# One layer of a hybrid SSD, RWKV-7 and PEER model: elementwise work of the RWKV branch moved from GpSimd to DVE and ACT

## The chip, the cores and the metric

The kernel runs on one core of a Trainium2 chip. The engines are named as in the profile: PE (TensorE; PEld is its loading of weights), DVE (VectorE), ACT (ScalarE), POOL (GpSimd) and SP, which issues most DMAs. The metric is the time of one execution in microseconds. Before the change the median of three runs is 3061.49 us (3054.85 to 3067.48).

## The reference

One inference step of a layer for a prompt of 512 tokens and eight sample tokens with states. All matrices are float32.

```python
h = rmsnorm(x, norm_mix)
z, xbc_raw, dt_raw, rw_proj, gate_m, gate_r = split_proj(h @ w_in)     # 1024 -> 11552 columns
y_m, ... = mamba_branch(z, xbc_raw, dt_raw, ...)                       # SSD scan, 32 heads of 64
y_r, ... = rwkv_branch(rw_proj, ...)                                   # RWKV-7, 16 heads of 64
x = x + (sigmoid(gate_m) * y_m + sigmoid(gate_r) * y_r) @ w_out
x = x + peer(rmsnorm(x, norm_ffn), ...)                                # 16384 experts
x = x + sigmoid(rmsnorm(x, norm_ple) @ w_ple_gate) * (p @ w_ple_proj)
```

The change lies in the RWKV branch. Its input is mixed with the row before, and then each head carries a 64 x 64 state through the tokens:

```python
xs = proj + (prev - proj) * shift_mu
r, k, v, xw, xa, xg = split(xs)
kk = normalised k * k_k ;  k = k * (1 + (a - 1) * k_a)
s = s * w + (s @ (-kk)) (x) (kk * a) + v (x) k ;   y = s @ r           # for every token
```

## The kernel before

The kernel goes through the layer in stages. Up to about 1180 us it projects `h @ w_in` in tiles of 128 columns and works off both branches from them; then come the output projections, and from about 1450 us PEER. Every float32 projection is made of three passes over split operands (`mm3`, L95 to L97): a weight tile `wraw` of 1024 x 128 is copied by ACT to `whi` (L78), DVE makes the rest `wlo` (L79), and PE runs 2 x 8 x 3 = 48 matmuls of 260 columns. `wraw`, `whi` and `wlo` have two buffers each, so a cast L78 can start only when PE has done the tile two before it.

The RWKV branch is worked through in eight groups of two heads, g = 0 to 7. In each, `rw_tile` (L413) makes r, k and v; `rwkv_in` (L518) makes the scaled vectors; `rwkv_inv` (L574) inverts small triangular blocks on DVE, in a loop over L598 and L601, with two round trips through DRAM to change the layout (the second is L602, a copy on ACT, then the DMAs L603 and L606); `rwkv_pre` (L615) does the chunk matrices; and `rwkv_chain` (L681) passes the state through eight chunks of 64 tokens. Sample tokens (`rwkv_s`, `ssd_s`) and the SSD branch (`ssd`) are interleaved with it, and projection tiles fill PE between them. Names that matter: `bb` = kk x a; `bk` = bb and k2 scaled by `di`, one instruction for each half of the partitions and each factor (L559, L560); `ck` the same with `de` (L561, L562); `di` and `dp` at L610 are the diagonal blocks and their transposes, which `mm4` (L513) takes at once; `AM` (L647, L671) is used by the chain.

A scheduler orders the instructions when the program is built: each engine gets one list, which it works off strictly in order, by estimated durations, priorities and the buffers at hand. A `pin` keeps an instruction in the order of the source. Moving an instruction to another engine therefore makes a new list on every engine.

Of the kernel before, what the change touches and what calls it, by code (L numbers as in the profile page):

```python
# [14 lines left out]
OP = mybir.AluOpType  # L15
# [15 lines left out]
def tile_hybrid(ctx: ExitStack, tc, x_prompt, x_sample, p_prompt, p_sample, state_ssm, state_conv,  # L31
# [7 lines left out]
    V, S, G, T = nc.vector, nc.scalar, nc.gpsimd, nc.tensor  # L39
# [373 lines left out]
    def rw_tile(j):  # L413

        ps = proj(W_RW + j * P, P, hT)
        raw = raw_of(ps, rwS[:, j], rtail[:, j:j + 1], 1)
        d = l2.tile([P, 2, NH], F32, name="dtmp").rearrange("p i t -> p (i t)")[:, :512]
        G.tensor_tensor(d, raw[:, 2:514], raw[:, 3:515], op=OP.subtract)
        xs = lp.tile([P, 512], F32, name=f"xs{min(j // 8, 2)}")
        V.scalar_tensor_tensor(xs, d, rows["shift_mu"][:, j:j + 1], raw[:, 3:515], op0=OP.mult, op1=OP.add)  # L420
        return xs
# [81 lines left out]
    def c8(t):  # L503
        return t.rearrange("p (c t) -> p c t", t=64)
# [13 lines left out]
    def rwkv_in(g, r, k, v, lw_):  # L518

        ps = pb()  # L520
        T.matmul(ps, lhsT=lw_[64:128, 1], rhs=xa[64:128], start=True, stop=True)
        a = full("a")
        S.activation(a, ps, AF.Tanh, scale=0.5, bias=rows["aaa_a0"][:, g:g + 1])
        S.activation(a, a, AF.Copy, scale=0.5, bias=0.5)
        ps = pb()
        for b in range(4):
            T.matmul(ps[:, b * P:(b + 1) * P], lhsT=xwaug[:, b * P:(b + 1) * P], rhs=lw_[0:65, 0], start=True, stop=True)
        lw = full("lw")
        S.activation(lw, ps, AF.Tanh, scale=0.5)
        S.activation(lw, lw, AF.Copy, scale=-0.5 * CDEC, bias=-0.5 * CDEC)  # L530
        dr, di, dp_, de = full("dr"), full("di"), full("dp"), full("de")
        for m, outs in ((cumI, ((dr, 1.0), (di, -1.0))), (cumS, ((dp_, 1.0),)), (cumC, ((de, 1.0),))):
            ps = pb()
            for b in range(4):
                T.matmul(ps[:, b * P:(b + 1) * P], lhsT=lw[:, b * P:(b + 1) * P], rhs=m, start=True, stop=True)
            for o, sg in outs:
                S.activation(o, ps, AF.Exp, scale=sg)
        drc = l2.tile([P, 8], F32, name="drc")
        V.tensor_copy(drc, dr[:, 63:512:64])

        sq = full("sq")
        S.activation(sq, k, AF.Square, scale=rows["k_k"][:, g:g + 1])
        ps = head_rs(sq, 1e-12, bd64, pb)
        kk = full("kk")
        V.scalar_tensor_tensor(kk, k, rows["k_k"][:, g:g + 1], ps, op0=OP.mult, op1=OP.mult)
        bb = full("bb")
        G.tensor_tensor(bb, kk, a, op=OP.mult)
        V.tensor_scalar(a, a, rows["k_a"][:, g:g + 1], omka[:, g:g + 1], op0=OP.mult, op1=OP.add)
        k2 = full("k2")
        V.tensor_tensor(k2, k, a, op=OP.mult)  # L550
        V.scalar_tensor_tensor(sq, r, rows["r_k"][:, g:g + 1], k2, op0=OP.mult, op1=OP.mult)
        ar = lp.tile([P, 8, 2, 64], F32, name="ar", bufs=2)
        V.scalar_tensor_tensor(ar[:, :, 0, :], c8(kk), -1.0, c8(dp_), op0=OP.mult, op1=OP.mult)
        V.tensor_tensor(ar[:, :, 1, :], c8(r), c8(dr), op=OP.mult)
        bk = lp.tile([P, 8, 2, 64], F32, name="bk")
        ck = lp.tile([P, 8, 2, 64], F32, name="ck")
        for e in range(2):
            sl = slice(64 * e, 64 * e + 64)
            V.tensor_tensor(bk[sl, :, e, :], c8(bb)[sl], c8(di)[sl], op=OP.mult)  # L559
            V.tensor_tensor(bk[sl, :, 1 - e, :], c8(k2)[sl], c8(di)[sl], op=OP.mult)  # L560
            G.tensor_tensor(ck[sl, :, e, :], c8(bb)[sl], c8(de)[sl], op=OP.mult)  # L561
            G.tensor_tensor(ck[sl, :, 1 - e, :], c8(k2)[sl], c8(de)[sl], op=OP.mult)  # L562
        return drc, sq, ar, bk, ck

    def bonus(sq, v):
# [8 lines left out]
    def rwkv_inv(g, ar, bk):  # L574

        L64 = c8(full("de"))
        lc16 = lp.tile([P, 8, 16], F32, name="lw")
        for hf in range(2):
            hs = slice(4 * hf, 4 * hf + 4)
            L = mm4(lambda ro, i: ar[ro, 4 * hf + i, 0, :], lambda ro, i: bk[ro, 4 * hf + i, ro.start // 64, :])  # L580
            V.tensor_tensor(L64[:, hs], L, b64(m64, 4), op=OP.mult)
            lm = c8(full("kk"))[:, 0:4]
            V.tensor_tensor(lm, L, b64(m16, 4), op=OP.mult)
            V.tensor_reduce(lc16[:, hs], lm.rearrange("p c (b k) -> p c k b", k=16), axis=AX.X, op=OP.add)
        ld, td = ld_d[g % 2], td_d[g % 2]
        nc.scalar.dma_start(ld.rearrange("c p k -> p c k"), lc16)
        yield
        lb = lp.tile([64, 16, 16], F32, name="a")
        pin(nc.sync.dma_start(lb.rearrange("q r k -> q (r k)"), ld.rearrange("c (z r) k -> (c z) (r k)", r=16)))
        yield  # L590
        tb = lp.tile([64, 16, 32], F32, name="sq")
        pin(V.memset(tb, 0.0))
        V.memset(tb.rearrange("p r k -> p (r k)")[:, 0:512:33], 1.0)
        tf = lp.tile([64, 16, 16], F32, name="k2")
        for j in range(15):
            tt = tf[:, j + 1:, 0:j + 1]
            sh = [64, 15 - j, j + 1]
            i = V.tensor_tensor(tt, lb[:, j + 1:, j:j + 1].to_broadcast(sh), tb[:, j:j + 1, 0:j + 1].to_broadcast(sh), op=OP.mult)  # L598
            if j == 0:
                pin(i)  # L600
            V.tensor_tensor(tb[:, j + 1:, 0:j + 1], tb[:, j + 1:, 0:j + 1], tt, op=OP.add)  # L601
        S.copy(tb[:, :, 16:32], tb[:, :, 0:16].rearrange("p r k -> p k r"))  # L602
        nc.scalar.dma_start(td.rearrange("c (z r) k -> (c z) (r k)", r=16), tb.rearrange("q r k -> q (r k)"))  # L603
        yield
        tc16 = lp.tile([P, 8, 32], F32, name="lw")
        pin(nc.scalar.dma_start(tc16, td.rearrange("c p k -> p c k")))  # L606
        yield
        T16, TT16 = c8(full("di")), c8(full("dp"))
        for q, (E_, t) in enumerate(((V, T16), (G, TT16))):
            pin(E_.tensor_tensor(t.rearrange("p c (b k) -> p c b k", k=16),  # L610
                                 tc16[:, :, None, 16 * q:16 * q + 16].to_broadcast([P, 8, 4, 16]),
                                 mb16[:, None].to_broadcast([P, 8, 4, 16]), op=OP.mult))
        yield L64, T16, TT16

    def rwkv_pre(g, v, ar, bk, ck, L64, T16, TT16):  # L615
# [21 lines left out]
        for hf in range(2):  # L637
# [30 lines left out]
                S.copy(uv[rv, e], pv[rv])  # L668
            for e in range(2):
                ro = slice(64 * e, 64 * e + 64)  # L670
                G.tensor_copy(AM[ro, e, :, 0:64], ar[ro, 4 * hf:4 * hf + 4, 0, :])  # L671
            out.append((AM, TT64, ctok, uv))
        return out

# [1042 lines left out]
```

## Time and profile before

| | |
|---|---|
| median of three runs | 3061.49 us |
| profiled execution | 3051.57 us |
| its span | 3049.9 us |
| PE busy | 2821.5 us (93%) |
| DVE busy | 2249.9 us (74%) |
| ACT busy | 988.6 us (32%) |
| POOL busy | 685.8 us (22%) |

Busy shares are taken over the whole span. [...] A line such as `PE psB L513 <- DVE bk L559` says that PE's instruction at L513, which writes psB, stood idle until DVE's instruction at L559, which writes bk, was done. In a timeline the brackets hold the idle time before an instruction and what ended it.

### The profile page before, as it was taken

What the parts mean: (1) busy time and instruction counts of PE and PEld (TensorE: products, weight loads), DVE (VectorE), ACT (ScalarE), POOL (GpSimd) and SP (SyncE); (2) the same over time, 40 slices, a digit from 0 to 9 for tenths busy, and PEclk for the clock granted to TensorE, in tenths of its full rate; (3) what the DMA queues carried; (4) which work ended last, traced back from release to release, by engine and by line L of the source; (5) the groups of instructions that cost most, each with busy time, mean ns of one, the idle gap of its engine ahead of it and who ended that gap; (6) DMA issues with size and microseconds to landing.
All of it is one profiled execution on the core that took longest, in us unless ns stands there. A gap on an engine that the chain in (4) does not pass through costs nothing. (4 is left out here: it accounts for less than half of the span.)

```text
span 3049.9 us, 52517 instructions
## 1 busy us (share of the span) xinstructions
PE 2821.5 (93%) x20188; PEld 2617.4 (86%) x20192; DVE 2249.9 (74%) x5375; ACT 988.6 (32%) x1995; POOL 685.8 (22%) x522
## 2 busy tenths in 40 slices
PE   5999999898897999998968989899999999999998
PEld 4878888777777888987968989898999999999986
DVE  5867767787777775334999999695677778878846
ACT  2333323333242322332223333232323343333332
POOL 0222231322314132210013121121222333432100
PEclk9999979998988999999989999999999999999999
DMA  3314242424334265632326768677998989988830
GB/s 87 78 41 105 76 103 60 113 60 104 73 87 113 68 153 158 198 112 93 90 61 198 245 203 245 211 241 230 315 334 303 328 302 327 337 326 313 287 119 29
DMA packets 446995, 528.15 MB, mean 173 GB/s; under 512 B 95464, under 2 KB 357243, under 8 KB 446705
## 3 DMA queue, kind: packets, MB, share of 16 engines
q1 hardware_dynamic: 386153, 377.42, 40.1%
q0 software_dynamic: 38304, 139.22, 13.5%
q10 hardware_dynamic: 22288, 8.16, 1.1%
q8 instruction: 159, 2.61, 0.4%
q14 instruction: 91, 0.75, 0.1%
HBM read 447.83 MB, written 77.14 MB: 172 GB/s over the span
## 5 line engine op out<-in xcount | busy, mean ns | idle before, releaser
L97 PE MATMUL ps<-hhi,wlo 128*128 128x260 f32 (+1 forms) x1456 | 444.6, 305 | 1.7 <-DVE wlo L79 1.7
L96 PE MATMUL ps<-hlo,whi 128*128 128x260 f32 (+1 forms) x1456 | 444.4, 305 | 0.0
L95 PE MATMUL ps<-hhi,whi 128*128 128x260 f32 (+1 forms) x1456 | 443.8, 305 | 0.6 <-DVE rsa L122 0.3
L97 PE MATMUL psA<-h2h,ul 128*128 128x392 f32 x1024 | 354.1, 346 | 24.8 <-DVE ul L1500 24.4
L95 PE MATMUL psA<-h2h,uh 128*128 128x392 f32 x1024 | 365.7, 357 | 0.2 <-ACT uh L1499 0.2
L96 PE MATMUL psA<-h2l,uh 128*128 128x392 f32 x1024 | 354.6, 346 | 0.0
L97 PE MATMUL av<-ah,vl 128*128 128x392 f32 x1024 | 351.5, 344 | 1.9 <-DVE vl L79 1.9
L95 PE MATMUL av<-ah,vh 128*128 128x392 f32 x1024 | 348.9, 341 | 3.3 <-ACT vh L78 3.2
L96 PE MATMUL av<-al,vh 128*128 128x392 f32 x1024 | 349.6, 341 | 0.9 <-DVE al L79 0.9
L95 PEld LDWEIGHTS ps<-hhi,whi 128*128 128x128 f32 (+1 forms) x1456 | 286.6, 197 | 13.9 <-issue 6.8
L96 PEld LDWEIGHTS ps<-hlo,whi 128*128 128x128 f32 (+1 forms) x1456 | 286.6, 197 | 12.7 <-issue 6.0
L97 PEld LDWEIGHTS ps<-hhi,wlo 128*128 128x128 f32 (+1 forms) x1456 | 286.3, 197 | 12.6 <-issue 4.0
L1453 POOL DMA_INDIRECT gr<-in_peer_v_dram,e x128 | 184.3, 1440 | 367.9 <-DVE o L1468 349.7
L1453 POOL DMA_INDIRECT gr<-in_peer_u_dram,e x128 | 125.3, 979 | 499.8 <-DVE junk L1462 448.2
L78 ACT CAST vh<-vr 128x1024 fp32r<-128x1024 f32 x128 | 134.3, 1051 | 315.8 <-PE av L96 121.3
L97 PEld LDWEIGHTS psA<-h2h,ul 128*128 128x128 f32 x1024 | 196.7, 192 | 27.4 <-DVE ul L1500 26.3
L78 ACT CAST whi<-wraw 128x1024 fp32r<-128x1024 f32 (+1 forms) x115 | 119.9, 1043 | 292.9 <-PE ps L96 250.5
L95 PEld LDWEIGHTS psA<-h2h,uh 128*128 128x128 f32 x1024 | 196.7, 192 | 0.9 <-ACT uh L1499 0.9
L96 PEld LDWEIGHTS psA<-h2l,uh 128*128 128x128 f32 x1024 | 197.3, 193 | 0.0
L79 DVE TENSOR_TENSOR vl<-vr,vh 128x1024 fp32r<-128x1024 f32 x128 | 156.2, 1222 | 55.4 <-ACT vh L78 52.2
L95 PEld LDWEIGHTS av<-ah,vh 128*128 128x128 f32 x1024 | 192.9, 188 | 3.9 <-ACT vh L78 3.5
L97 PEld LDWEIGHTS av<-ah,vl 128*128 128x128 f32 x1024 | 192.9, 189 | 2.5 <-DVE vl L79 2.5
(635 smaller groups left out, 6498.9 us busy)
## 6 DMA issues: line engine op xcount, KB each, us to landing
ur<-in_peer_u_dram SPq DMA_DIRECT2D x128, 512.0 KB
vr<-in_peer_v_dram SPq DMA_DIRECT2D x128, 512.0 KB
wraw<-in_w_in_dram SPq DMA_DIRECT2D x90, 512.0 KB
Gt<-G_d SPq DMA_DIRECT2D x32, 784.0 KB
G_d<-stg SPq DMA_DIRECT2D x12, 2048.0 KB
ge_d<-ge SPq DMA_DIRECT2D x112, 196.0 KB
gl<-ge_d SPq DMA_DIRECT2D x112, 196.0 KB
wraw<-in_w_out_ssm_dram SPq DMA_DIRECT2D x16, 512.0 KB
```

Source lines behind the costliest of these rows:

```text
L78: S.copy(hi, raw)
L79: eng.tensor_tensor(lo, raw, f(hi), op=OP.subtract)
L95: T.matmul(out, lhsT=a[0], rhs=b[0], start=start, stop=False)
L96: T.matmul(out, lhsT=a[0], rhs=b[1], start=False, stop=False)
L97: T.matmul(out, lhsT=a[1], rhs=b[0], start=False, stop=stop)
L1453: pin(G.indirect_dma_start(out=t, out_offset=None, in_=(peer_u, peer_v)[s_ // P][0], in_offset=bass.IndirectOffsetOnAxis(ap=e3[:, s_ % P:s ...
```

## The change

Six places of the RWKV branch change engine. DVE now makes the difference of the shifted rows (L418, 26 times), `bb` (L547, 8 times), `ck` (L561 and L562, 32 times) and `dp` (L610, 8 times); ACT makes the copies into `AM` (L671, 32 times). POOL keeps its work on the sample tokens (L836, L837, L842, L916, L920) and of the SSD branch (L994, L1008).

```diff
--- before.py
+++ after.py
@@ -415,7 +415,7 @@
         ps = proj(W_RW + j * P, P, hT)
         raw = raw_of(ps, rwS[:, j], rtail[:, j:j + 1], 1)
         d = l2.tile([P, 2, NH], F32, name="dtmp").rearrange("p i t -> p (i t)")[:, :512]
-        G.tensor_tensor(d, raw[:, 2:514], raw[:, 3:515], op=OP.subtract)
+        V.tensor_tensor(d, raw[:, 2:514], raw[:, 3:515], op=OP.subtract)
         xs = lp.tile([P, 512], F32, name=f"xs{min(j // 8, 2)}")
         V.scalar_tensor_tensor(xs, d, rows["shift_mu"][:, j:j + 1], raw[:, 3:515], op0=OP.mult, op1=OP.add)
         return xs
@@ -544,7 +544,7 @@
         kk = full("kk")
         V.scalar_tensor_tensor(kk, k, rows["k_k"][:, g:g + 1], ps, op0=OP.mult, op1=OP.mult)
         bb = full("bb")
-        G.tensor_tensor(bb, kk, a, op=OP.mult)
+        V.tensor_tensor(bb, kk, a, op=OP.mult)
         V.tensor_scalar(a, a, rows["k_a"][:, g:g + 1], omka[:, g:g + 1], op0=OP.mult, op1=OP.add)
         k2 = full("k2")
         V.tensor_tensor(k2, k, a, op=OP.mult)
@@ -558,8 +558,8 @@
             sl = slice(64 * e, 64 * e + 64)
             V.tensor_tensor(bk[sl, :, e, :], c8(bb)[sl], c8(di)[sl], op=OP.mult)
             V.tensor_tensor(bk[sl, :, 1 - e, :], c8(k2)[sl], c8(di)[sl], op=OP.mult)
-            G.tensor_tensor(ck[sl, :, e, :], c8(bb)[sl], c8(de)[sl], op=OP.mult)
-            G.tensor_tensor(ck[sl, :, 1 - e, :], c8(k2)[sl], c8(de)[sl], op=OP.mult)
+            V.tensor_tensor(ck[sl, :, e, :], c8(bb)[sl], c8(de)[sl], op=OP.mult)
+            V.tensor_tensor(ck[sl, :, 1 - e, :], c8(k2)[sl], c8(de)[sl], op=OP.mult)
         return drc, sq, ar, bk, ck
 
     def bonus(sq, v):
@@ -606,7 +606,7 @@
         pin(nc.scalar.dma_start(tc16, td.rearrange("c p k -> p c k")))
         yield
         T16, TT16 = c8(full("di")), c8(full("dp"))
-        for q, (E_, t) in enumerate(((V, T16), (G, TT16))):
+        for q, (E_, t) in enumerate(((V, T16), (V, TT16))):
             pin(E_.tensor_tensor(t.rearrange("p c (b k) -> p c b k", k=16),
                                  tc16[:, :, None, 16 * q:16 * q + 16].to_broadcast([P, 8, 4, 16]),
                                  mb16[:, None].to_broadcast([P, 8, 4, 16]), op=OP.mult))
@@ -668,7 +668,7 @@
                 S.copy(uv[rv, e], pv[rv])
             for e in range(2):
                 ro = slice(64 * e, 64 * e + 64)
-                G.tensor_copy(AM[ro, e, :, 0:64], ar[ro, 4 * hf:4 * hf + 4, 0, :])
+                S.copy(AM[ro, e, :, 0:64], ar[ro, 4 * hf:4 * hf + 4, 0, :])
             out.append((AM, TT64, ctok, uv))
         return out
 
```

The lists of all engines are new. The first place is DVE at `bk` in g=4, before:

```order
L545 SCALAR_TENSOR_TENSOR kk<-xs_6564,VB,psB 128x512
L988 SCALAR_TENSOR_TENSOR x_6818<-x_6818,dsk,psA 128x128
L553 SCALAR_TENSOR_TENSOR ar<-kk,dp 128x8x64
L548 TENSOR_SCALAR a<-a,VB,omka 128x512
L559 TENSOR_TENSOR bk<-bb,di 64x8x64
L550 TENSOR_TENSOR k_6715<-xs_6564,a 128x512
L559 TENSOR_TENSOR bk<-bb,di 64x8x64
L551 SCALAR_TENSOR_TENSOR sq<-xs_6469,VB,k_6715 128x512
L560 TENSOR_TENSOR bk<-k_6715,di 64x8x64 x2
```

And now (`x` and `raw` are tiles of the SSD branch and of the projections):

```order
L545 SCALAR_TENSOR_TENSOR kk<-xs_6564,VB,psB 128x512
L988 SCALAR_TENSOR_TENSOR x_6947<-x_6947,dsk,psA 128x128
L547 TENSOR_TENSOR bb<-kk,a 128x512
L553 SCALAR_TENSOR_TENSOR ar<-kk,dp 128x8x64
L548 TENSOR_SCALAR a<-a,VB,omka 128x512
L559 TENSOR_TENSOR bk<-bb,di 64x8x64
L550 TENSOR_TENSOR k_6715<-xs_6564,a 128x512
L561 TENSOR_TENSOR ck<-bb,de 64x8x64
L551 SCALAR_TENSOR_TENSOR sq<-xs_6469,VB,k_6715 128x512
L560 TENSOR_TENSOR bk<-k_6715,di 64x8x64
L562 TENSOR_TENSOR ck<-k_6715,de 64x8x64
L559 TENSOR_TENSOR bk<-bb,di 64x8x64
```

`bb` now stands in DVE's list, and three of the four `ck` before the second L559. On PE the first two matmuls of L513 need the first L559 alone, the other 14 rows the second. Between the two pieces stand 13, 14, 13, 13, 8, 8, 8 and 8 projection matmuls in g = 0 to 7 before; now they are 33, 27, 21, 28, 28, 28, 28 and 28.

The second place is `dp` in g=5. Before, it stands on POOL (`sH` are sample tokens):

```order
L836 TENSOR_TENSOR sH<-sH,sB 128x512
L837 TENSOR_TENSOR sH<-sB,s_x_8302 128x512
L842 TENSOR_TENSOR sH<-sH 128x512
L610 TENSOR_TENSOR dp<-lw,mb_270 128x512
L916 TENSOR_TENSOR sH<-sB,s_dx 128x1024
L920 TENSOR_TENSOR sH<-sH,sB 128x1024
```

Now it stands on DVE:

```order
L79 TENSOR_TENSOR wlo<-wraw,whi 128x1024
L834 TENSOR_TENSOR sH<-sH,sB 128x512
L610 TENSOR_TENSOR di<-lw,mb_270 128x512
L835 TENSOR_REDUCE s_sa<-sH 128x8
L610 TENSOR_TENSOR dp<-lw,mb_270 128x512
L838 TENSOR_TENSOR sH<-sB,s_sa 128x512
L777 TENSOR_TENSOR s_x_9774<-shS,rwS 128x24
```

It no longer has L842 ahead of it; L835, a sample instruction, stands between `di` and `dp`. The third place is ACT ahead of this, in g=5, the end of the round trip that gives `di` and `dp` their input. Before:

```order
L78 CAST whi<-wraw 128x1024
L408 COPY raw_556<-ps 128x512
L409 COPY xbcS<-ps 128x8
L410 COPY ctail<-ps 128x3
L602 COPY sq<-sq 64x16x16
L603 DMA td_d_86<-sq 64x512
L606 DMA lw<-td_d_86 128x8x32
L78 CAST whi<-wraw 128x1024
```

And now:

```order
L78 CAST whi<-wraw 128x1024
L408 COPY raw_556<-ps 128x512
L409 COPY xbcS<-ps 128x8
L410 COPY ctail<-ps 128x3
L78 CAST whi<-wraw 128x1024
L602 COPY sq<-sq 64x16x16
L603 DMA td_d_86<-sq 64x512
L606 DMA lw<-td_d_86 128x8x32
L630 COPY bb<-psB 128x256
```

One more cast L78 stands ahead of L602. In g = 4, 5 and 6 it was the 54th, 63rd and 72nd cast and is the 55th, 64th and 73rd, and the matmuls on `dp` stand behind 54, 63 and 72 whole projection tiles in both programs. A cast starts when the tile two before it is done. Thus 96 projection matmuls stood between that moment and the matmuls on `dp`, and now 48 do; in g=3 they were 80 and are 48. In g=3 and g=6 the split L79 of that very cast also stands ahead of the last L601 on DVE. In g=3 the last steps of the reciprocal root for L1020 (L122 to L124) stood behind `di` on DVE, and now they stand ahead of it. In g = 2, 3 and 6 L843 stands ahead of L632 on DVE, a few rows behind `dp`. The DMA lists keep the same transfers.

## Rows read from the trace of the kernel before

**Rows 1.** Busy time by stage: us, each engine's busy us (instructions), clock, DMA.
```profile
100.00:1180.00 1080.00, 988.83 (x8743) 857.07 (x8747) 804.26 (x2022) 358.73 (x924) 282.34 (x209) 0.92 0.36 90
```

**Rows 2.** PE's waits, 100 to 1180 us: total, times, longest.
```profile
PE psB L513 <- POOL dp L610: 23.2, 6, 6.7
...
PE psB L513 <- DVE bk L559: 22.8, 13, 3.2
...
PE psA L1020 <- DVE rsy L124: 5.6, 2, 5.3
...
PE psB L655 <- ACT ctok L657: 1.6, 3, 0.5
```

**Rows 3.** Groups of POOL's instructions: count, busy us, mean ns, idle before.
```profile
L418 POOL TENSOR_TENSOR dtmp<-raw 128x512 f32<-128x512 f32 x26 | 41.6, 1600 | 149.0 <-ACT raw L408 77.0 <-ACT rwS L409 35.7 <-ACT rtail L410 25.3
...
L562 POOL TENSOR_TENSOR ck<-k,de 64x512 f32<-64x512 f32 x16 | 29.3, 1832 | 9.0 <-DVE k L550 8.6
...
L671 POOL COPY AM<-ar 64x256 f32<-64x256 f32 x32 | 22.7, 710 | 29.4 <-DVE AM L647 23.6 <-DVE yS L925 4.8 <-DVE rsa L122 0.6
...
L561 POOL TENSOR_TENSOR ck<-bb,de 64x512 f32<-64x512 f32 x16 | 22.2, 1388 | 0.9
...
L547 POOL TENSOR_TENSOR bb<-kk,a 128x512 f32<-128x512 f32 x8 | 12.6, 1569 | 156.0 <-DVE kk L545 156.0
```

**Rows 4.** Groups of DVE's instructions, the same columns.
```profile
L559 DVE TENSOR_TENSOR bk<-bb,di 64x512 f32<-64x512 f32 x16 | 19.1, 1196 | 0.2
...
L554 DVE TENSOR_TENSOR ar<-xs,dr 128x512 f32<-128x512 f32 x8 | 5.5, 685 | 0.0
```

**Rows 5.** Groups of ACT's instructions, the same columns.
```profile
L668 ACT COPY uv<-psB 64x256 f32<-64x256 f32 x32 | 11.7, 366 | 10.5 <-PE psB L665 10.2
```

**Rows 6.** Timeline of g=4 at bk: start, us, engine, instruction, idle before.
```profile
648.50 0.75 DVE L545 SCALAR_TENSOR_TENSOR kk<-xs,VB,psB 128x512 f32<-128x512 f32 x1 [0.66 <-PE psB L493]
...
649.39 1.28 POOL L547 TENSOR_TENSOR bb<-kk,a 128x512 f32<-128x512 f32 x1 [5.07 <-DVE kk L545]
...
649.55 1.67 DVE L553 SCALAR_TENSOR_TENSOR ar<-kk,dp 128x512 f32<-128x512 f32 x1
...
652.57 1.74 DVE L559 TENSOR_TENSOR bk<-bb,di 64x512 f32<-64x512 f32 x1
...
654.36 0.33 PE L513 MATMUL psB<-bk,ar 64*64 64x64 f32 x2 [2.32 <-DVE bk L559]
```

**Rows 7.** Timeline of g=4 at dp.
```profile
686.21 1.05 ACT L78 CAST whi<-wraw 128x1024 fp32r<-128x1024 f32 x1 [7.57 <-PE ps L96]
...
687.16 0.67 ACT L602 COPY sq<-sq 64x256 f32<-64x256 f32 x1
...
694.75 0.69 DVE L610 TENSOR_TENSOR di<-lw,mb 128x512 f32<-128x512 f32 x1 [4.92 <-DMA lw<-td_d]
...
701.68 1.26 POOL L842 TENSOR_TENSOR sH<-sH 128x512 f32<-128x512 f32 x1 [1.68 <-issue]
...
702.90 1.26 POOL L610 TENSOR_TENSOR dp<-lw,mb 128x512 f32<-128x512 f32 x1
...
704.21 0.48 PE L513 MATMUL psB<-dp,de 64*64 64x64 f32 x4 [5.50 <-POOL dp L610]
```

**Rows 8.** Busy time by stage, short stretches.
```profile
509.00:522.00 13.00, 10.25 (x63) 8.25 (x62) 11.53 (x15) 2.13 (x5) 7.61 (x5) 0.61 0.03 6
...
563.00:591.00 28.00, 24.55 (x270) 21.21 (x271) 17.53 (x25) 7.32 (x16) 10.31 (x8) 0.76 0.59 170
...
688.00:697.00 9.00, 9.00 (x77) 9.00 (x76) 4.08 (x6) 1.58 (x4) 0.00 (x0) 1.00 0.51 74
...
1052.00:1058.00 6.00, 5.13 (x48) 4.81 (x49) 5.92 (x6) 0.00 (x0) 3.67 (x3) 0.72 0.01 3
...
415.00:447.00 32.00, 31.51 (x262) 27.46 (x263) 16.53 (x35) 6.80 (x18) 9.80 (x9) 0.52 0.31 83
...
703.00:731.00 28.00, 22.95 (x247) 20.38 (x248) 21.08 (x30) 9.01 (x22) 13.80 (x9) 0.57 0.62 176
```

## The prediction

> **What bounds the kernel now.** I read the view by stages first. The stage that the change touches, from 100 to 1180 us, has PE busy for 988.83 of 1080 us [rows 1]: TensorE bounds it, and DVE (804.26) and POOL (282.34) matter only where PE waits for them. [...] After the stage PE is just as full, so what is won in it should come out of the total one to one.
>
> Then the waits of PE in that stretch [rows 2]. Two lines hold half of the idle time: the matmuls of L513 wait 23.2 us for dp (POOL, L610) and 22.8 us for bk (DVE, L559). Next is L1020 behind DVE's small operations, 5.6 us. The groups of POOL and DVE [rows 3, 4] give the prices, and the timelines of g=4 [rows 6, 7] say why PE waits.
>
> At bk: kk ends at 649.25, bb takes POOL 1.28 us, and beside POOL's products DVE's own instructions stretch: ar takes 1.67 us and bk 1.74, where a DVE product of the same kind takes 0.685 us [rows 4]. bk is done 5.8 us after kk started, and PE stood 2.32 us [rows 6]. At dp: the cast of L78 on ACT waits 7.57 us for PE to leave its buffer; L602 comes behind it, then two DMAs, and di starts on DVE at 694.75, 8.54 us after the cast began. Its twin dp starts only at 702.90, because POOL takes its queue in order and L842 stands ahead, which needs DVE's late L840. PE waits 5.50 us [rows 7].
>
> **The change part by part.** POOL loses 26 differences (41.6 us), 8 bb (12.6), 32 ck (29.3 + 22.2), 32 copies (22.7) [rows 3] and 8 dp at 1.26 [rows 7], together 138 us. DVE gets 74 of these at about 0.685 us [rows 4], some 50 us, and ACT 32 copies at 0.366 [rows 5], 11.7 us. DVE's busy time has a counter-entry: bk alone took 1196 ns where 685 would do [rows 4], 16 x 0.51 = 8 us, and ar, a, sq and k2 beside it stretch in the same way. I book DVE's load as about unchanged. None of it is a term by itself; terms are where PE waits.
>
> 1. *bk.* On DVE the row from kk to the first bk is kk, one small instruction, bb, ar, a, bk: 0.75 + 0.35 + 4 x 0.69 = 3.9 us instead of 5.8, so the 2.32 us of g=4 go. The second bk (the other half of the partitions) comes behind five more products and itself: 6 x 0.69 = 4.1 us. The order now puts 28 projection matmuls between the two pieces of L513, where 8 to 14 stood; at 9.00/77 = 0.117 us each [rows 8] they cover 3.3 us, and two more matmuls a little. A wait of 0.3 to 0.6 us per g is left, 2 to 5 us of the 22.8. Bounds: 0 (ck pushes the second bk out as far as bb pulls in the first) and -22.8. I take **-19 us**.
>
> 2. *dp.* The stall behind L842 goes, and I ask what is late next. In both orders L602 stands behind a cast that needs PE to have finished an earlier projection tile (48 matmuls). Before, two tiles lay between that point and dp's matmuls in g=4 to 6; now it is one, in g=3 to 6. The chain from the cast to di was 8.54 us [rows 7] and nothing in it is moved; di, L835 and dp add 3 x 0.69, so dp is ready 10.6 us after the point, and PE arrives after 48 x 0.117 = 5.6 us. It waits 5.0 us, and 6.2 where DVE's 1.22 us split also stands ahead of L601 (g=3, g=6): some 22 us in four groups, and a few in g=1 and 2, against 23.2. The wait changes its name from POOL to DVE and stays. Bounds: -23 (the DMAs come sooner) and +25 (they come later). I take **+1 us**.
>
> 3. *L1020.* Its wait in g=3 was 5.3 of the 5.6 us [rows 2]. There the last steps of its reciprocal root stood behind di on DVE, and so behind di's DMA; now they stand ahead. **-4 us**, between 0 and -5.6.
>
> 4. *Copies on ACT.* Row: ACT copies 64x256 in 366 ns [rows 5], POOL took 710 on average [rows 3]. But each copy waits for AM on DVE and holds up ctok, for which PE already waits 1.6 us at one line [rows 2]. Bounds: -2 (waits on POOL's copies go) and +8 (two thirds of the 11.7 us come to PE). I take **+2 us**.
>
> [...] With the copies at no cost either way the sum would be 2 us lower.
>
> 5. *L632.* In g=2, 3 and 6 L843 now stands ahead of L632 at a time when its input, L842 (1.26 us on POOL [rows 7]), is not ready. About 1.3 us in three groups: **+4 us**, between 0 and +8.
>
> 6. *Clock.* [...] Not all of it will return, since short gaps stay: **-13 us** (0 to -18). Behind the dp gap of g=2 there are 31 us at half clock (0.52 over 32 us), the longest of the stage [rows 8]; a shorter gap may or may not bring it: **-4 us** (0 to -15). And g=3 gets a dp gap like that of g=4: 0.57 over 28 us there against 0.76 in g=3 now [rows 8], 0.19 x 28 = 5 us: **+5 us**.
>
> Sum: -19 + 1 - 4 + 2 + 4 - 13 - 4 + 5 = **-28 us**. The 26 differences are at nothing: DVE has 276 idle us in the stage [rows 1], PE waits for none of them in rows 2, and on DVE they take half of POOL's 1600 ns [rows 3]; without that cover they would cost 26 x 0.685 = 18 us, spread out. The profiled execution took 3051.57 us (span 3049.9), which gives 3023.6. It lies 9.9 us below the median of the three runs, 3061.49, so I forecast 3061.5 - 28 = **3033 us** for the median.
>
> **Rivals.**
> *No change.* The bk gain is eaten: ck lies between the two bk pieces, the half clock finds other gaps. For it: DVE is busy 5.92 of 6 us there [rows 8], and terms 2 and 6 show how gaps move rather than vanish. Against it: 28 projections now cover. With -19 + 13 given back the time is 3055; chance 0.21.
> *More than forecast.* dp's chain comes 3 us sooner (POOL's neighbours no longer stretch DVE's work ahead of L601) and the half clock behind it goes: -12 and -15 more, 3006. For it: 138 us leave POOL. Against: PE meets dp a tile earlier. Chance 0.12.
> *Slower: the round trip to dp.* PE reaches dp's matmuls one tile after the gating cast, so each us by which DVE finishes L601 late is a us of idle PE. DVE now has the differences and splits between the small steps of that loop. If dp waits 8.5 us in seven groups, that is 60 - 23 = +37, some 12 more at half clock, less the 36 of terms 1, 3 and 6: +13, 3075. It decides from an average wait of some 7 us. Chance 0.07.
> *Slower: DVE becomes the bound.* Where bk is made DVE has no idle time at all [rows 8]. If its instructions stay at 1.2 us although POOL has gone quiet, the five products added there come on top, 5 x 0.69 = 3.4 us in each of eight groups, 27 us, less 20 more projections of cover (2.3 us) in seven of them, 16: +11 in place of -19. With the half clock kept and one us for each g in the chain behind, +19: 3080. Chance 0.04. [...]
>
> **How the numbers follow.** The forecast has 0.56, with a range of its own of 3015 to 3048. About 0.5% of the time, 15 us, is what can be told from no change. Below 3046 lie nine tenths of the forecast, all of the larger gain and a little of no change: 0.65. Above 3077 lie most of the two slow cases: 0.10. The rest is 0.25. The range of 8 in 10 reaches from the larger gain to the no-change case and its scatter: 3005 to 3068.
>
> **What would show it.** Right: bk (L559) at 0.67 to 0.75 us each and its wait on PE under 6 us; the dp wait, now on DVE, at some 4 to 7 us in g=3 to 6 with a cast and L602 close ahead of it; the stage's clock above 0.93 on average and no half clock at the first bk gap. Wrong: a dp wait over 40 us or under 8, bk still over 1 us, or a stage that shortens by less than 10 us although rows 2's two lines shrink.

## The result, and the profile after

The changed kernel takes 3007.44 us (median of four runs, 3000.47 to 3012.05) against 3058.17 for the kernel before on the same chip: a ratio of 0.9835 [0.9802, 0.9867], some 50 us less. A second timing gave 3003.53 us and 0.9816 [0.9793, 0.9839], 56 us. The forecast was 3033 us, 28 less; the time lies inside the range and below the likeliest case's own.

The page of the profiled execution (3006.43 us, span 3004.7; busy us, share of the span, instructions):

```profile
PE 2791.0 (93%) x20187; PEld 2592.2 (86%) x20192; DVE 2230.3 (74%) x5449; ACT 1000.3 (33%) x2027; POOL 536.1 (18%) x416
```

The clock granted to PE is 0.962 of full speed on average over the span, 0.954 before. Its record has two values in both executions, 1.00 and 0.50, here called full and half clock.

DVE took over 74 instructions (5375 before) and is busy for 20 us less than before, 2230.3 against 2249.9. The groups of the instructions moved, and of `bk` (count, busy us, mean ns, idle before), say why:

```profile
L418 DVE TENSOR_TENSOR dtmp<-raw 128x512 f32<-128x512 f32 x26 | 17.7, 679 | 0.0
...
L562 DVE TENSOR_TENSOR ck<-k,de 64x512 f32<-64x512 f32 x16 | 10.9, 684 | 0.0
L559 DVE TENSOR_TENSOR bk<-bb,di 64x512 f32<-64x512 f32 x16 | 10.9, 683 | 0.1
...
L547 DVE TENSOR_TENSOR bb<-kk,a 128x512 f32<-128x512 f32 x8 | 5.5, 687 | 0.1
```

Each of these products takes 0.68 us on DVE, as booked from [rows 4]; only `dp` (L610) takes longer, 0.80 us on average. `bk` fell from 1196 ns to 683 with no edit of its own, because POOL's `ck` no longer runs beside it. The runs below show that it is `ck`: with `ck` on DVE and the differences, `dp` and the copies still on POOL (e1) `bk` takes 684 ns, and with `ck` back on POOL it takes 1215 (e5) and 1206 (e10, `bb` back as well).

The stretch that [rows 1] show for before ends some 50 us sooner, so 100 to 1130 us answers to 100 to 1180 (the same columns: PE, PEld, DVE, ACT, POOL busy with counts, then the clock). Behind it stand the places of [rows 8]: `dp` in g=2, `bk` in g=3, `dp` in g=3, `bk` in g=7, and then the small matmuls behind `dp` in g=5.

```profile
100.00:1130.00 1030.00, 961.93 (x8746) 836.47 (x8750) 786.24 (x2086) 372.31 (x957) 154.10 (x108) 0.94 0.39 95
405.00:437.00 32.00, 30.46 (x359) 26.18 (x357) 26.64 (x55) 13.59 (x33) 11.37 (x5) 1.00 0.58 157
490.00:503.00 13.00, 13.00 (x119) 11.54 (x117) 10.91 (x23) 2.18 (x7) 0.00 (x0) 1.00 0.05 14
533.00:561.00 28.00, 20.35 (x233) 17.92 (x234) 22.20 (x39) 11.57 (x28) 7.85 (x4) 0.56 0.58 161
1002.00:1008.00 6.00, 6.00 (x69) 5.65 (x68) 5.99 (x11) 1.20 (x2) 0.00 (x0) 1.00 0.12 47
793.00:802.50 9.50, 7.33 (x146) 6.73 (x147) 7.58 (x18) 1.66 (x4) 3.16 (x2) 0.85 0.64 176
```

PE makes the same matmuls (some 8700), with 68.07 us idle instead of 91.17 and busy for 961.93 us instead of 988.83. So 23 us came from waits and 27 from the clock, 50 in all; the rest of the program takes 5 us more in this execution (1874.7 us against 1869.9). Both `bk` places, at half clock in part before (0.61 and 0.72), are at 1.00. The place behind `dp` in g=2 went from 0.52 to 1.00, and that in g=3 fell from 0.76 to 0.56.

PE's waits in this stretch (total, times, longest; answers to [rows 2]):

```profile
PE psB L513 <- DVE dp L610: 19.0, 4, 5.2
PE psB L711 <- DVE X L707: 5.6, 5, 2.0
PE psB L717 <- ACT uv L713: 5.3, 7, 1.2
...
PE psB L655 <- DVE AM L647: 4.2, 8, 0.9
PE psB L513 <- DVE bb L632: 4.1, 4, 1.7
...
PE psA L1020 <- DVE rsy L124: 0.6, 1, 0.6
```

`bk` is not in the list any more. `dp` has its new name and nearly its old size, and L1020 is gone but for 0.6 us. What has grown are small waits in the state chain: L711, L717 and L655 on AM together 15.1 us, before 6.0. The timeline of g=4 at `bk` (start, us, engine, instruction, idle before), which answers to [rows 6]:

```profile
616.88 0.75 DVE L545 SCALAR_TENSOR_TENSOR kk<-xs,VB,psB 128x512 f32<-128x512 f32 x1
...
617.93 0.68 DVE L547 TENSOR_TENSOR bb<-kk,a 128x512 f32<-128x512 f32 x1
618.53 0.68 DVE L553 SCALAR_TENSOR_TENSOR ar<-kk,dp 128x512 f32<-128x512 f32 x1
...
619.59 0.68 DVE L559 TENSOR_TENSOR bk<-bb,di 64x512 f32<-64x512 f32 x1
```

kk, `bb`, `ar` and `bk` follow one another on DVE; from kk's start to the end of the first `bk` it is 3.4 us, where it was 5.8, and PE has no wait there. And at `dp` in g=4, which answers to [rows 7]:

```profile
651.62 1.05 ACT L78 CAST whi<-wraw 128x1024 fp32r<-128x1024 f32 x1 [5.28 <-PE ps L96]
652.84 0.68 ACT L602 COPY sq<-sq 64x256 f32<-64x256 f32 x1 [0.17 <-DVE sq L601]
...
660.54 0.69 DVE L610 TENSOR_TENSOR di<-lw,mb 128x512 f32<-128x512 f32 x1 [6.57 <-DMA lw<-td_d]
661.15 0.68 DVE L610 TENSOR_TENSOR dp<-lw,mb 128x512 f32<-128x512 f32 x1
...
661.89 0.62 PE L513 MATMUL psB<-dp,de 64*64 64x64 f32 x14 [4.44 <-DVE dp L610]
```

L602 stands a cast later, the cast waits for PE as before, `di` and `dp` follow one another, and PE waits 4.44 us for the whole round trip instead of 5.50 for L842.

### The profile page after: what moved, and what is told of

It is laid out like the page before. It is cut to its first block, busy times and chain, and to the rows that moved or that the text cites. A ratio compares the mean times of both kernels' runs of the same rounds, so it can differ in the third digit from the quotient of the medians.

```text
span 3004.7 us, 52438 instructions
## 1 busy us (share of the span) xinstructions
PE 2791.0 (93%) x20187; PEld 2592.2 (86%) x20192; DVE 2230.3 (74%) x5449; ACT 1000.3 (33%) x2027; POOL 536.1 (18%) x416
## 3 DMA queue, kind: packets, MB, share of 16 engines
q0 software_dynamic: 38304, 139.22, 13.7%
## 5 line engine op out<-in xcount | busy, mean ns | idle before, releaser
L97 PE MATMUL ps<-hhi,wlo 128*128 128x260 f32 (+1 forms) x1456 | 435.3, 299 | 0.0
L1453 POOL DMA_INDIRECT gr<-in_peer_v_dram,e x128 | 172.0, 1344 | 384.2 <-DVE o L1468 366.4
L78 ACT CAST vh<-vr 128x1024 fp32r<-128x1024 f32 x128 | 134.3, 1051 | 316.1 <-issue 108.0
L78 ACT CAST whi<-wraw 128x1024 fp32r<-128x1024 f32 (+1 forms) x115 | 120.0, 1043 | 277.7 <-PE ps L96 232.3
L96 PEld LDWEIGHTS av<-al,vh 128*128 128x128 f32 x1024 | 192.9, 188 | 4.0 <-DVE al L79 4.0
```

The lines of the kernel that those rows point to most:

```text
L78: S.copy(hi, raw)
L96: T.matmul(out, lhsT=a[0], rhs=b[1], start=False, stop=False)
L97: T.matmul(out, lhsT=a[1], rhs=b[0], start=False, stop=stop)
L1453: pin(G.indirect_dma_start(out=t, out_offset=None, in_=(peer_u, peer_v)[s_ // P][0], in_offset=bass.IndirectOffsetOnAxis(ap=e3[:, s_ % P:s ...
```

## The experiments

The half clock is read from the trace's record of the granted clock, piece by piece, from the first projection matmul (33 us) to the last L752, the end of the stage. Idle time of PE is taken over the same stretch. Ratios stand against the kernel before on the same chip; one per cent is 30.6 us.

| kernel | ratio [95%] | us against before | stage, us | PE idle | half clock |
|---|---|---|---|---|---|
| before | 1 | 0 | 1132 | 100 | 171 |
| changed | 0.9835 [0.9802, 0.9867] | -50 | 1082 | 76 | 116 |
| e1 bb, ck alone | 0.9887 [0.9871, 0.9903] | -35 | 1099 | 90 | 140 |
| e2 dp alone | 0.9954 [0.9930, 0.9978] | -14 | 1112 | 94 | 147 |
| e3 differences alone | 0.9915 [0.9900, 0.9929] | -26 | 1104 | 97 | 126 |
| e4 copies alone | 1.0023 [1.0004, 1.0041] | +7 | 1132 | 102 | 188 |
| e5 changed, ck back | 0.9884 [0.9860, 0.9907] | -35 | 1097 | 87 | 116 |
| e10 changed, bb and ck back | 0.9914 [0.9897, 0.9931] | -26 | 1106 | 92 | 119 |
| e6 changed, dp back | 0.9915 [0.9897, 0.9933] | -26 | 1109 | 95 | 171 |
| e7 changed, differences back | 0.9855 [0.9832, 0.9879] | -44 | 1083 | 76 | 102 |
| e8 changed, copies back | 0.9863 [0.9839, 0.9888] | -42 | 1086 | 78 | 119 |
| e11 changed, late differences back | 0.9862 [0.9842, 0.9883] | -42 | 1098 | 76 | 147 |
| e12 loop first | 0.9887 [0.9864, 0.9910] | -35 | 1100 | 76 | 140 |
| e13 changed, dp's wait filled | 0.9834 [0.9812, 0.9857] | -51 | 1094 | 65 | 96 |
| e14 changed, filled behind dp | 0.9872 [0.9849, 0.9895] | -39 | 1096 | 66 | 96 |
| e15 before, g=2's wait filled | 0.9958 [0.9940, 0.9976] | -13 | 1123 | 101 | 133 |
| e16 changed, again | 0.9816 [0.9793, 0.9839] | -56 | 1086 | 79 | 140 |

The first two columns are from all runs, the last three from one profiled execution, which can lie some us from the median (e13's is the slowest of its five). What is left of the span outside the stage is 1917 to 1934 us in these executions, and 3 to 6 us apart for the same program, so a difference of some 10 us between two kernels need not lie in the stage. In e4, e6 and e16 some 17 us of the half clock are part of a piece at the start of the program that the other executions don't have.

### Each part alone

**e1.** `bb` and `ck`:

```diff
-        G.tensor_tensor(bb, kk, a, op=OP.mult)
+        V.tensor_tensor(bb, kk, a, op=OP.mult)
-            G.tensor_tensor(ck[sl, :, e, :], c8(bb)[sl], c8(de)[sl], op=OP.mult)
-            G.tensor_tensor(ck[sl, :, 1 - e, :], c8(k2)[sl], c8(de)[sl], op=OP.mult)
+            V.tensor_tensor(ck[sl, :, e, :], c8(bb)[sl], c8(de)[sl], op=OP.mult)
+            V.tensor_tensor(ck[sl, :, 1 - e, :], c8(k2)[sl], c8(de)[sl], op=OP.mult)
```

> Only bb and ck go to DVE (L547, L561, L562); the differences, dp and the copies stay on POOL. PE's order has 28 projection matmuls between the two pieces of L513 at bk, as in the changed kernel. Theory A (the gain is made at bk: PE's waits there, and the half clock that follows them): the bk wait falls from 22.8 us to under 3, the 37 us of half clock at the eight bk gaps go, -20 and -18: about 3020 us. dp's wait stays on POOL behind L842 at 5 to 7 us a group. Theory B (POOL and DVE slow one another, and the gain goes with POOL's time moved, 64 of 138 us): 3035 us. Theory C (only the whole change gives the new order): 3048 to 3068 us.

3025.46 us. The `bk` wait is gone and none of the half-clock pieces lies at a `bk` gap, as A has it. Idle time fell by 10 us and PE's busy time by 23, where A had 20 and 18. The idle time falls short because `dp`, still behind L842 on POOL, now keeps PE waiting longer:

```profile
PE psB L513 <- POOL dp L610: 35.9, 6, 8.4
```

The 31 us piece behind `dp` in g=2 is gone as well, which A had not named, and between `bk` in g=3 and `bk` in g=7 the half clock away from the `bk` gaps grew from 89 us to 126. So that the time comes near to A's figure is in part luck.

**e2.** `dp`:

```diff
-        for q, (E_, t) in enumerate(((V, T16), (G, TT16))):
+        for q, (E_, t) in enumerate(((V, T16), (V, TT16))):
```

> Only dp goes to DVE (L610). bk stays as it was. In g = 4 to 6 there are 88 projection matmuls between the point that starts the gating cast and dp's matmuls, 10.3 us against a chain of 10.6. Theory A: dp's wait falls from 23.2 us to under 8 and takes its half clock along, some -16 and -10; bk's wait stays near 22.8 us: about 3032 us. Theory B (10 of 138 us of POOL's time): 3054 us. Theory C: 3048 to 3068 us.

3042.53 us. PE's wait for `dp` is down to 2.2 us and that for `bk` stays at 23.7. But half of A's -26 came: idle time fell by 6 us only, with small waits behind `dp` grown (L655 on AM 5.6 us, L711 5.4), and half-clock pieces of 14 to 20 us still lie behind `dp` in g = 4, 5 and 6, though no wait for `dp` of more than 0.5 us precedes them. Most of the half clock that went (24 us) is the piece in g=2, 10 us here instead of 31.

**e3.** The differences:

```diff
-        G.tensor_tensor(d, raw[:, 2:514], raw[:, 3:515], op=OP.subtract)
+        V.tensor_tensor(d, raw[:, 2:514], raw[:, 3:515], op=OP.subtract)
```

> Only the 26 differences go to DVE (L418). Theory A: nothing of it stands before a wait of PE; bk and dp keep their waits: 3050 to 3062 us. Theory B (41.6 of 138 us): 3043 us. Theory C: 3048 to 3068 us.

3033.45 us: A is refuted. All three theories priced it too low. The two big waits are still there:

```profile
PE psB L513 <- POOL dp L610: 29.9, 7, 8.0
PE psB L513 <- DVE bk L559: 22.8, 10, 3.1
```

Idle time fell by 3 us only, half clock by 44. The 31 us piece behind `dp` in g=2 (0.52 in [rows 8]) is a 3.4 us piece here; the same 32 us have

```profile
413.00:445.00 32.00, 31.23 (x354) 26.43 (x354) 26.91 (x57) 10.40 (x27) 12.96 (x9) 0.95 0.54 149
```

**e4.** The copies:

```diff
-                G.tensor_copy(AM[ro, e, :, 0:64], ar[ro, 4 * hf:4 * hf + 4, 0, :])
+                S.copy(AM[ro, e, :, 0:64], ar[ro, 4 * hf:4 * hf + 4, 0, :])
```

> Only the 32 copies into AM go to ACT (L671). PE's order stays nearly that of before. Theory A: +2 us as forecast for this term, 3055 to 3062 us. Theory B (22.7 of 138 us): 3050 us. Theory C: 3048 to 3068 us.

3067.92 us, 7 slower: a loss as A had it, and larger. B falls: with POOL's time it would go the other way, and e3 gave more than its share. The four parts alone add up to -68 us, the whole gives 50 to 56: they overlap, and C's figure holds for none but e4. One thing that they share can be named: the piece of 31 us behind `dp` in g=2 is gone in e1 and is 10 us in e2, 3.4 in e3 and 14 here, behind a wait of 2.67 us.

### Each part put back

**e5.** `ck` back on POOL in the changed kernel (L561, L562; `V` to `G`).

> The changed kernel with ck back on POOL (L561, L562); bb stays on DVE. PE's order has 8 to 13 projection matmuls between the two pieces of L513 at bk again, where the changed kernel has 21 to 33. Theory A (POOL's ck stretches DVE's bk beside it, and the projections that cover bk are gone): some of bk at 1.2 to 1.8 us in place of 0.69, the bk wait back at 8 to 20 us with half clock behind it: 3020 to 3032 us. Theory B (gain by POOL's time moved, ck is 51 of 138 us): 3026 us, with bk's wait gone. If bk needs only bb on DVE: 3005 to 3012 us.

3029.01 us, as A has it in time and wait; the half clock, which A also had coming back, stays at 116 us, with 7 of it at `bk` gaps. B's 3026 us is near too, but B had `bk`'s wait gone. `bk` beside POOL's `ck` and its wait:

```profile
L559 DVE TENSOR_TENSOR bk<-bb,di 64x512 f32<-64x512 f32 x16 | 19.4, 1215 | 0.2
```

```profile
PE psB L513 <- DVE bk L559: 12.6, 9, 1.8
```

**e10.** `bb` as well as `ck` back on POOL.

> The changed kernel with bb and ck back on POOL (L547, L561, L562): only the differences, dp and the copies are moved. Theory A (the gain sits at bk): the bk wait is back at 20 to 25 us, with its half clock: 3030 to 3040 us. Theory F (the parts overlap in the same places, any two of them give most of it): 3012 to 3025 us.

3033.39 us, A's case, and F is refuted: `bk`'s wait is 23.5 us again. So this part is worth 24 to 30 us as the last one added, and 35 as the first.

**e6.** `dp` back on POOL.

> The changed kernel with dp back on POOL (L610). dp stands behind L842 there again; 48 projection matmuls lie between the point that frees the gating cast and dp's matmuls in g = 3 to 6. Theory A (dp on DVE hides a wait that would be worse now, since the other parts took away a tile of cover): the dp wait goes from 19.0 to some 35 to 50 us: 3022 to 3035 us. If the move of dp is worth nothing beside the others: 3005 to 3012 us.

3033.39 us, A's case:

```profile
PE psB L513 <- POOL dp L610: 38.0, 6, 9.7
```

Alone `dp` gave 14 us, beside the others it gives 24 to 30: the other parts take away one projection tile of its cover, and only on DVE does it stand that.

**e7.** The differences back on POOL.

> The changed kernel with the 26 differences back on POOL (L418). Alone they gave 25 us, against nothing in the forecast. Theory D (a gain of their own, at places the other parts don't touch): 3030 to 3036 us. Theory A (the gain overlaps with that of bk: both remove the long stretch at half clock and the wait of L1020 in g=2 and 3): 3005 to 3015 us.

3016.13 us, just above A's range and far from D's. Alone they gave 26 us, here 6 to 12. Their gain is for the most part the one that the other parts make too, and of the 6 to 12 us none is seen in the stage: it takes 1083 us here (in the fastest of the four executions) and 1082 and 1086 in the two profiles of the changed kernel. `dp` waits only 5.3 us here. In g = 3 and 4 it has more cover (72 and 95 projections); in g = 5 and 6, with the same 48, it waits 1.8 and 2.1 us instead of 4.2 and 5.2. There L418 no longer stands among the small steps of the loop L598 to L601, and from the cast to `di` it is 6.3 and 6.6 us instead of 8.1 and 9.1.

**e8.** The copies back on POOL.

> The changed kernel with the 32 copies into AM back on POOL (L671). The list of PE is the same as in the changed kernel. Theory A (the copies on ACT hold up ctok and cost 2 to 7 us, as when moved alone): 3000 to 3005 us, with a shorter wait of L655 and L711. Theory B (22.7 of 138 us of POOL's time): 3015 us. Less than 2 us either way means that the copies don't matter.

3017.75 us: the sign is B's. With the same list of PE, the copies on ACT gain 8 to 14 us here, where alone they cost 7. L655 and L711 do not wait longer with them on POOL (3.4 and 4.0 us, against 4.2 and 5.6). The gain is not in these waits. Nor is it in the stage, which takes 1086 us here and 1082 and 1086 in the two profiles of the changed kernel. Where it lies is open.

### The same program again

**e0.** The kernel before, unchanged.

> The kernel before once more, for a second profile of the same program. [...]

174 us at half clock (stage 1134 us, PE idle 102), where the first profile has 171, and the 31 us piece behind `dp` in g=2 again: what belongs to the order of the work would repeat like this, and in these two executions it does. The piece, in the same 32 us counted from the wait:

```profile
417.50:449.50 32.00, 31.43 (x260) 27.35 (x261) 16.85 (x36) 6.78 (x18) 10.16 (x10) 0.52 0.31 83
```

**e16.** The changed kernel, unchanged.

> The changed kernel once more, unchanged. If copies and differences are each worth 6 to 8 us beside the other parts: 3004 to 3011 us, ratio to before 0.982 to 0.985. If they are worth nothing there: 3013 to 3018 us, ratio near 0.986. The profile: idle time of PE up to the last L752 within 5 us of 75 and half clock within 10 us of 116, if both belong to the order of the work.

0.9816, and 3003.53 us: by the time, copies and differences are worth something beside the others; in the stage it is not seen. Idle time (79) repeats, and so do the half-clock pieces of g = 3 to 6 to within 3.4 us. But the sum of the half clock, 140 us, misses the 116 by more than the 10 expected. Two pieces are longer: one of 24 us at the start of the program, and one behind `dp` in g=7, 27.3 us here and 3.4 in the first profile, behind the same wait of 1.7 us (for `bb`, L632).

### Taking the rest of dp's wait away

**e11.** From g = 3 on the differences are on POOL:

```diff
-        V.tensor_tensor(d, raw[:, 2:514], raw[:, 3:515], op=OP.subtract)
+        (V if j >= 24 or j % 8 < 3 else G).tensor_tensor(d, raw[:, 2:514], raw[:, 3:515], op=OP.subtract)
```

> The changed kernel with the differences on DVE for the two tiles 24 and 25 and for g = 0 to 2 alone; from g = 3 on they are on POOL again. Theory G (on DVE the late differences stand between the small steps of the loop L598 to L601 and lengthen the chain to dp by 2 to 3 us a group, while the early ones help before g = 2): the dp wait falls from 19.0 us to under 8, and the time is 8 to 15 us below the changed kernel's, 2992 to 3000 us. If the dp wait is a matter of cover alone: 3003 to 3012 us, with a dp wait only where 48 projection matmuls cover it (g = 5 and 6, 5 us each).

3019.85 us. The first half of G holds, with 6.3 us of `dp` wait; the second does not: the time is 8 to 14 us above that of the changed kernel, not below. PE is idle for 76 us all the same, and the half clock is 147 us instead of 116.

**e12.** The differences on DVE for g = 0 and 1 alone, and the loop ahead of all else:

```diff
+        (V if j >= 24 or j % 8 < 2 else G).tensor_tensor(d, raw[:, 2:514], raw[:, 3:515], op=OP.subtract)
+        tf = lp.tile([64, 16, 16], F32, name="k2"); hp = ExitStack(); hp.enter_context(tc.high_priority(600))
...
+        nc.scalar.dma_start(td.rearrange("c (z r) k -> (c z) (r k)", r=16), tb.rearrange("q r k -> q (r k)")); hp.close()
```

> The differences on DVE for tiles 24, 25 and g = 0 and 1 alone, and the loop L598 to L601 with its copy L602 at a high priority. 88 to 92 projection matmuls cover the chain to dp in g = 2 to 6. [...] Theory H (the half clock behind dp belongs to the stretch of small matmuls itself): the wait goes and the half clock stays at 70 us or more: 2990 to 3003 us.

3028.13 us, far above H's range. PE's waits:

```profile
PE psB L711 <- DVE X L707: 10.4, 12, 2.0
PE psB L717 <- ACT uv L713: 7.4, 11, 1.2
PE psB L513 <- DVE dp L610: 6.1, 4, 2.9
...
PE psB L655 <- DVE AM L647: 5.7, 6, 2.7
```

13 us of `dp`'s wait are gone, but PE is idle for 76 us as in the changed kernel: the state chain behind `dp` waits instead. And there are 140 us at half clock instead of 116.

### Filling the wait

**e13.** Ahead of `dp`'s matmuls in g = 3 to 6, PE gets matmuls whose results nobody reads:

```diff
+        pv = ps[:, 0:256].rearrange("p (c t) -> p c t", t=64); [tc.keep_in_program_order(T.matmul(ps[:, 256:512], lhsT=hhi[:, n % 8, 0, 0:128], rhs=hhi[:, n % 8, 1, 0:256], start=True, stop=True)) for n in range(int(hold))]
...
+            S.copy(WT[hf], mm4(ih(L64, hf), ih(TT16, hf), (36 if g in (3, 4, 5, 6) else 0.5) if hf == 0 else 0))
```

> The changed kernel with 36 additional matmuls of 256 columns (L509), whose results nobody reads, ahead of dp's matmuls in g = 3 to 6: 36 x 0.115 = 4.1 us of work in each, in place of a wait of 4.2 to 5.2. Theory G (the wait brings the half clock on): dp's wait below 2 us in sum and the half clock of g = 3 to 6, 92 us now, below 40: some -25 us, 2980 to 2990 us. Theory H (the stretch of small matmuls has it in any case): 70 us or more stay, 3000 to 3012 us.

3009.74 us; H. The list changes as well: 66 to 76 projections lie between the gating cast and `dp`'s matmuls, where the changed kernel has 48. The wait is down to 3.5 us, and of the 92 us at half clock in g = 3 to 6 some 70 to 75 stay. Two stretches of g=5 (busy time, clock), `dp`'s small matmuls first, then those of L655, L711 and L717:

```profile
798.00:812.50 14.50, 12.77 (x203) 10.86 (x203) 11.34 (x23) 4.57 (x10) 5.89 (x4) 1.00 0.63 189
813.00:831.00 18.00, 12.92 (x85) 10.67 (x86) 14.13 (x20) 5.44 (x15) 5.07 (x3) 0.53 0.43 118
```

The first is at full clock with 0.6 us of wait ahead; in the changed kernel, with 4.18 us of wait ahead, it had 0.85 (793 to 802.5 us above). The second is at half clock all the same.

**e14.** The matmuls between the small ones, in g = 3 to 6:

```diff
+        pv = ps[:, 0:256].rearrange("p (c t) -> p c t", t=64); [T.matmul(ps[:, 256:512], lhsT=hhi[:, n % 8, 0, 0:128], rhs=hhi[:, n % 8, 1, 0:256], start=True, stop=True) for n in range(fill)]
...
+            S.copy(WT[hf], mm4(ih(L64, hf), ih(TT16, hf), hf == 0, fill=6 if 3 <= g <= 6 else 0))
```

(and the same `fill` at the other three calls of `mm4` in `rwkv_pre`).

> The changed kernel with 6 additional matmuls of 256 columns ahead of each of the eight groups of small ones (L513) behind dp in g = 3 to 6: 48 x 0.115 = 5.5 us in each, 22 us in all. In g = 4 to 6 dp also has 96 projection matmuls of cover. Theory H: between wide matmuls the half clock of this stretch falls from 92 us to under 45, -24 us, and the additional work costs 5 to 15 us beside the waits: 2990 to 3005 us. Theory G: the half clock goes only where dp's wait goes, and does so in e13 as well. If neither: half clock as before and +10 to +22 us, 3015 to 3030 us.

3018.46 us: neither G nor H, but the last line, the additional work. The same two stretches of g=5:

```profile
800.00:818.00 18.00, 16.11 (x220) 13.89 (x220) 12.71 (x24) 5.21 (x12) 6.97 (x4) 1.00 0.74 204
820.00:834.00 14.00, 9.49 (x69) 7.44 (x65) 11.50 (x20) 6.22 (x20) 2.93 (x1) 0.51 0.31 84
```

H named the wrong small matmuls. Those directly behind `dp` are at full clock where the wait ahead of them is short (in g=5 0.6 us in e13, 1.5 here). The half clock lies on what follows them: transposes for ctok and the first steps of the state chain, where PE is busy for 9.49 of 14 us, in bursts between waits for DVE and ACT of up to 1.1 us. It does not come with these steps everywhere: in g=3 of e5, e7 and e10, where 61 to 65 projection matmuls stand among them in the 16 us from the first L655 on, the clock is 1.00. No run filled these steps in g = 4 to 6, so what brings their clock down is argued and not shown. The bursts can't be the whole of it either: in the piece in g=2 before, PE was busy for 31.51 of 32 us [rows 8].

**e15.** The kernel before with 20 such matmuls in g=2 alone (the edit of e13, `20 if g == 2`).

> The kernel before with 20 additional matmuls of 256 columns (L509) ahead of dp's matmuls in g = 2 alone, 2.3 us, where PE waits 2.55 us. Theory G: the piece of 31 us at half clock behind it goes or falls below 12 us: -10 to -15 us, 3043 to 3050 us. Theory H: the piece stays within 20 to 35 us, 3055 to 3062 us.

3045.61 us, in G's range of time. `dp`'s wait in g=2 is 1.8 us, and the piece of 31 us is one of 14, between what G (under 12) and H (20 to 35) expected. That the wait brings the piece on is not shown by this: in e4 it is 14 us as well behind a wait of 2.67, and in e11 it is 17 us with no wait for `dp` ahead. The list also changes in g = 3 and 4, so not all of the 13 us need come from this piece.

## Why the prediction was right in its direction and short in its size

**The step that failed is term 6, the clock**: "-13 us" for the `bk` gaps and "-4 us" for what lies behind the `dp` gap of g=2. Place by place, us at half clock, before and after:

| place | before | after | worth | forecast |
|---|---|---|---|---|
| eight `bk` gaps | 37.5 | 0 | -19 | -13 |
| behind `dp`, g=2 | 30.7 | 0 | -15 | -4 |
| g=3, `dp` and behind | 13.7 | 27.3 | +7 | +5 |
| g = 4 to 6, `dp` and behind | 64.9 | 64.9 | 0 | 0 |
| other places | 23.9 | 23.9 | 0 | 0 |

That is 55 us, and half of it 27; PE's busy time fell by 26.9. So of the 22 us that the forecast of 28 lacks to the 50 of the stage, 15 are the clock's (27 for 12) and 7 the waits' (23 for 16). The repeats give the same shares: from e0 to e16 the stage falls by 48 us, 23 of idle and 25 of busy time. No run shows the -13 us of the eight `bk` places: they are 37.5 us at half clock before and none after, which is 19, one more than the forecast's own bound of 18. It took less on the ground that short gaps stay, and none stayed there (e1 shows it for this part alone). At g=2 it took 4 of the 15 us that it had itself put as the bound. e0 shows the piece again at its full length, with the order of the work the same. In every other program, whatever was moved, no piece there is longer than 17 us. So its 15 us go for the most part with any new list; nothing in the forecast says why the changed kernel should lose them whole, and that it does is luck, as far as is known. The piece was nearly twice as long as any other of the stage, and its 15 us were more than any single wait there (6.7 us at most).

**Term 1, bk**: right, -22.8 for -19. No wait is left at the second `bk`, behind its 21 to 33 projections. **Term 2, dp**: right in what it named: the wait changed its name, stands in g = 3 to 6 and is 4.2 to 5.2 us there, forecast 5.0 to 6.2; 19.0 in all for 24.2. From the cast to `di` it is 8.1 to 9.1 us there, forecast 8.54. e6 (38.0 us) shows the cover argument from the other side. **Term 3, L1020**: -5.0 for -4. **Term 5, L632**: the waits named in g = 2, 3 and 6 came, 2.5 us for 4; in all the wait for `bb` went from 2.3 us (`PE psB L513 <- DVE bb L632: 2.3, 2, 1.7` before) to 4.1.

**Term 4, copies**: forecast +2. Alone they cost 7 (e4), beside the other parts they gain 8 to 14 by the time (e8) and nothing that shows in the stage. The row of a copy, 366 ns forecast and 404 measured, says nothing of either. **The 26 differences**, forecast at nothing: alone -26 (e3), beside the other parts 6 to 12 by the time (e7), again not in the stage. The reason given, that no wait of PE in [rows 2] names them, was true and not enough: what they changed is the order around g = 2 and 3, and with it a half-clock piece that stands in no list of waits. Against "nothing in it is moved", they also lengthen `dp`'s chain: the wait is 19.0 us with them and 5.3 in e7, of which 5.5 are the longer chain in g = 5 and 6 and the rest lies in g = 3 and 4, where the cover changes too. But e11 and e12 show that this wait, once taken away, comes back elsewhere.

**Terms 1 to 5 together** were -16 us of idle time, measured -23: the waits that they name fell by 30, and the state chain's small waits, in no term, took 9 back. The gains of the parts alone don't add up to that of the whole: parts that remove the same piece share it.

**Rivals.** "More than forecast" came in its sum (3006) and in half of its mechanism: the half clock behind `dp` went in g=2, the `dp` chain came no sooner. "No change" falls with the `bk` wait, which is gone. "DVE becomes the bound" is refuted by the 0.68 us rows; "the round trip to dp" did not decide, at 4 to 5 us a group.

**Open** is what sets how long a half-clock piece lasts once it has begun: behind `dp` in g=2 it was 31 us before, 14 in e4 and 3.4 in e3, with waits of 2.55, 2.67 and 2.24 us ahead, and 17 in e11 with none; in g=7 it was 3.4 and 27.3 us in two executions of the same program. No version here beats the changed kernel: e13 equals it.

## What to carry over

Where the bounding engine's clock varies, list its half-clock pieces beside its waits and price them by the same care: here they were half of the gain, and a part that hardly touched a wait (3 us of idle time) gained 26 us, most of it through them. A shared piece is paid out once (the parts alone add up to -68 us, the whole gives 50 to 56), so parts of a change are timed both alone and as the last one added. And taking away a wait in a chain of small matmuls was worth nothing here where the next links came no sooner: 13 us of `dp`'s wait went in e11 and in e12, and PE was idle for 76 us all the same.

## What had not been expected of the hardware

- PE stayed at half clock for 31 us while it was busy for 31.51 of 32 us [rows 8], with 35 projection matmuls among some 225 small ones, behind a wait of 2.55 us; in two executions alike. In g=7 of e16 it did so for 27.3 us, busy for 27.0, and in another execution of the same program for 3.4.
- DVE's total busy time fell when 74 instructions were moved to it, because POOL's neighbours had stretched its own: `bk` 1196 to 683 ns (1215 in e5, with `ck` back on POOL), and the six groups of L548 to L551, L553, L559 and L560 together 79.3 to 42.9 us.
- Small matmuls by themselves did not lower the clock: right behind `dp` they ran at 1.00 where the wait ahead was short (g=5: 0.6 us in e13, 1.5 in e14).
